# Turned results for latent and cross attention in a two-layer hybrid decoder trunk

## The chip, the cores and the metric

The kernel runs on one core of a Trainium2 chip. The metric is the device time of one execution in microseconds (us). Three timed runs of the kernel before lie between 2052.78 and 2055.78 us, with a median of 2054.7 us. All arithmetic is float32 or a float32 value split into two fp32r parts.

## The reference

Two layers work on a residual stream of 512 tokens by 1024 features. Each layer has three attention branches that are gated and summed, and a squared-ReLU MLP.

```python
h = rmsnorm(x, g_mix[l])
dq, dk, dv, c_q, c_kv_kr, xq, gate_logits = jnp.split(h @ w_in[l], split_idx, axis=-1)
y_diff = diff_attention(...) @ w_diff_o[l]      # 8 heads, two maps a head, values 128 wide, causal
y_mla = latent_attention(...) @ w_mla_o[l]      # 8 heads, q and k 96 wide, values 64 wide, causal
y_mem = memory_cross_attention(...) @ w_cross_o[l]   # 4 heads, 128 wide, 256 memory tokens
x = x + (sig(g0) * y_diff + sig(g1) * y_mla + sig(g2) * y_mem) @ w_out[l]
x = x + jnp.square(jax.nn.relu(rmsnorm(x, g_mlp[l]) @ w_mlp1[l])) @ w_mlp2[l]
```

In each attention `p = softmax(q k^T * scale)` over the keys and `o = p v`. The change touches how `o` is made in latent attention (called mla in the kernel) and in cross attention; differential attention keeps its way.

## The kernel before

**Tiling.** Tokens are cut into four blocks of 128 (`NT = 4`, `P = 128`). Large products are made in split form: an operand is held as `hi`, its value rounded to fp32r, and `lo`, the rest; `mm3` (L108 to L111) makes three fp32r matmuls, hi·hi, hi·lo and lo·hi, into one PSUM bank. A split takes one ScalarE copy for `hi` (L101 or, with a scale, L105) and one VectorE subtraction for `lo` (L102 or L106). Weights stream in by SyncE DMAs of up to 512 KB and are split the same way in `do_split`. Attention products (L609, L612, L638, L642) are partly plain float32: the trace shows a plain float32 matmul as two instructions, each with its own weight load, and a transpose as one.

**Order.** `layer(l)` makes a list of entries. `phases` (L850) holds the attention units of a stage, `PLAN` (L25) the projections that stand beside them, and `merge` (L45) deals the two out in turn. Stage 1 has the first two pairs of latent heads (`mla_att(0)`, `mla_att(1)`) beside four gate products (`gx`) and the memory projection (`mem`). Stage 2 has the other two pairs beside `xq` and the first differential pair `d0`. Stage 3 has the four cross heads beside `d1` and `ym`. The framework then orders the instructions of each engine ahead of time, by priority and by its own model of durations; on the chip every engine runs its list in that fixed order and waits on semaphores.

**Attention before.** `attend` (L596) serves all three kinds. It makes the scores of two maps into PSUM (`ps("s")`), masks them, takes the negated maximum, and writes `exp` with its row sums into a tile `P` (L626). Then blocks of 128 by 128 of `P` are transposed on TensorE into a bank of `ps("tp")` (L638), copied out by ScalarE into a `PT` tile (L640, which is L95), and each block is the stationary operand of a plain float32 matmul whose moving operand is a block of values (L642): 64 columns wide for latent heads, 128 for cross and differential ones. The result has tokens on the partitions. After a head (cross) or a pair of heads (latent) `o_copy` (L659) copies the 512 columns out, `o_finish` (L644) divides by the row sums on VectorE (L646), transposes the result back in four blocks (L649) and splits it into fp32r `hi` and `lo` for the output projection.

**Values before.** `kvb_item` (L483) writes the values of four latent heads as one float32 tile for each two token blocks (L494, VectorE), `mem_chunk` the memory values likewise (L364, ScalarE).

**Buffers.** Tile pools at L72 to L74: `B` has 22 slots of 128 by 512 and holds, among others, latent keys and queries (four slots each for half the heads), values, the latent `ckv` and `cq`, memory inputs, keys and values, `xq` and the differential operands. `PT` has 2 slots, `P` 2, `ps("tp")` 2 and `ps("o")` 1. A tile's first write waits until a slot is free.

Of the kernel before, what the change touches and what calls it, by code (L numbers as in the profile page):

```python
# [59 lines left out]
def tile_trunk(ctx: ExitStack, tc: tile.TileContext, x_t, mem_t, mem_n, pos, ifr, gcol, grow, w_ck, w_cq, w_kvb, w_qb,  # L60
# [11 lines left out]
    pools = {n: pool(n, b) for n, b in (("H", 16), ("O", 16), ("X", 8), ("G", 1), ("B", 22), ("scr", 5), ("PT", 2))}  # L72
    p_p = pool("P", 2)
# [34 lines left out]
    def mm3(o, l, r, first, last):  # L108
        T.matmul(o, lhsT=l[0], rhs=r[0], start=first, stop=False)  # L109
        T.matmul(o, lhsT=l[0], rhs=r[1], start=False, stop=False)  # L110
        T.matmul(o, lhsT=l[1], rhs=r[0], start=False, stop=last)  # L111
# [28 lines left out]
    def trig():  # L140
# [44 lines left out]
        G.dma_start(out=lvt.rearrange("p (l d) -> p l d", l=L), in_=grow[:, 128:384].partition_broadcast(P))  # L185
# [93 lines left out]
    def layer(l):  # L279
# [58 lines left out]
        def mem_chunk(c):  # L338
            def done(tp, q):
# [143 lines left out]
        def kvb_item(hf):  # L483
            def fn(w):
                kn = [tl("O") for _ in range(2)]
                vv = [tl("B") for _ in range(2)]
                kc = []
                for t in range(NT):
# [5 lines left out]
                    V.tensor_scalar(vv[t // 2][:, sl], q[:, 256:512], s["skv"][:, t:t + 1], None, ALU.mult)  # L494
# [101 lines left out]
        def attend(N, qk, causal, o_out, ssum, vs, diff):  # L596
# [30 lines left out]
            nb = N // P  # L627
# [5 lines left out]
            blocks = [(m, j) for m in range(1 if diff else 2) for j in range(nb)]  # L633
            for i in range(0, len(blocks), 4):
                bl = blocks[i:i + 4]
                tp_ = ps("tp")
                for n, (m, j) in enumerate(bl):
                    T.transpose(tp_[:, n * P:(n + 1) * P], in_=pt[:, m, j * P:(j + 1) * P], identity=ident)  # L638
                w = tl("PT")
                copy_to(w[:, :len(bl) * P], tp_[:, :len(bl) * P])  # L640
                for n, (m, j) in enumerate(bl):
                    T.matmul(o_out[m], lhsT=w[:, n * P:(n + 1) * P], rhs=vs[m](j), start=j == 0, stop=j == nb - 1)  # L642
# [334 lines left out]
```

## Time and profile before

| what | value |
|---|---|
| three timed runs, median | 2054.7 us |
| the same, lowest and highest | 2052.78 and 2055.78 us |
| span of the profiled execution, first to last instruction | 2047.5 us |
| TensorE busy | 2025.8 us, 99% of the span |
| weight loads busy | 1735.7 us, 85% |
| VectorE busy | 1125.5 us, 55% |
| ScalarE busy | 870.5 us, 43% |

What lies around the span is not recorded for the profiled execution; the median of the timed runs is 7.2 us above its span. Matmuls are pipelined and their ends are modelled, so the duration in a row says how long one is in the array, and the distance from one start to the next says what it costs. PE in the rows is the TensorE matmul, PEld its weight load, DVE is VectorE, ACT is ScalarE, POOL is GpSimd, and an engine name with a q is its queue issuing a DMA.

### The profile page before, as it was taken

To read this page: it belongs to the slowest core of one execution; us is meant where nothing else is said; L and a number is where in the kernel's file an instruction comes from. 1 tells how busy PE (TensorE), PEld (TensorE's weight loads), DVE (VectorE), ACT (ScalarE), POOL (GpSimd) and SP (SyncE) were. 2 spreads that over 40 slices of the span, in tenths; PEclk is the share of its full clock that TensorE was granted. 3 is DMA by queue.
4 is the path that set the end of the run, shared out by engine and by line. 5 is a ranking of instruction groups with operands and counts; after the bars stand their busy time and mean duration, and the time that the engine had idled before them with its cause. 6 is when DMAs were issued, how large, how long until landed. Compare 5 with 4: busy or idle time off the path is not lost.

```text
span 2047.5 us, 28283 instructions
## 1 busy us (share of the span) xinstructions
PE 2025.8 (99%) x11280; PEld 1735.7 (85%) x11280; DVE 1125.5 (55%) x2058; ACT 870.5 (43%) x1607; POOL 152.4 (7%) x125
## 2 busy tenths in 40 slices
PE   8999999999999999999999999999999999999999
PEld 7889997888878888888888999978897788888887
DVE  7754665667656443443457546657685554434442
ACT  6565543444443442322345645444454334323221
POOL 2300110101100000000003001101020000000000
PEclk9999999999999999999999999999999999999999
DMA  5242122222214333333333321212222233333332
GB/s 178 78 140 74 63 65 60 73 73 63 73 48 150 96 97 94 102 93 101 118 95 94 115 72 63 67 58 73 73 63 63 92 124 93 94 102 93 101 94 73
DMA packets 54036, 181.09 MB, mean 88 GB/s; under 512 B 6176, under 2 KB 6704, under 8 KB 53904
## 3 DMA queue, kind: packets, MB, share of 16 engines
q1 hardware_dynamic: 51840, 175.66, 28.0%
q10 hardware_dynamic: 1872, 3.21, 0.5%
q8 instruction: 89, 1.46, 0.3%
q0 software_dynamic: 192, 0.41, 0.1%
q14 instruction: 43, 0.35, 0.1%
HBM read 175.06 MB, written 4.19 MB: 88 GB/s over the span
## 4 chain that ended last, share of the span: by engine, by line
PE 97%; ACT 1%; DMA 1%; DVE 1%; issue 0%; SPq 0%; POOL 0%; POOLq 0%; ACTq 0%
PE psacc L109 21%; PE psacc L110 20%; PE psacc L111 20%; PE pss L109 7%; PE pss L110 7%; PE pss L111 7%; PE pso L642 4%; PE pss L609 3%; PE pss L612 2%; PE pstp L638 2%; PE pstp L649 1%; PE pstp L590 1%; PE pstp L478 1%; DMA X<-in_x_t_dram 0%; DMA B<-in_mem_n_dram 0%; PE pstp L236 0%
## 5 line engine op out<-in xcount | busy, mean ns | idle before, releaser
L101 ACT ACTIVATE whi<-wraw 128x1024 fp32r<-128x1024 f32 (+3 forms) x320 | 334.5, 1047 | 726.8 <-PE psacc L110 354.5
L102 DVE TENSOR_TENSOR wlo<-wraw,whi 128x1024 fp32r<-128x1024 f32 (+3 forms) x320 | 386.0, 1207 | 103.1 <-ACT whi L101 101.8
L109 PE MATMUL psacc<-H,whi 128*128 128x512 f32 x816 | 322.0, 395 | 1.3 <-ACT B L560 1.3
L110 PE MATMUL psacc<-H,whi 128*128 128x512 f32 x816 | 321.1, 393 | 0.0
L111 PE MATMUL psacc<-H,wlo 128*128 128x512 f32 x816 | 319.6, 392 | 0.0
L109 PE MATMUL psacc<-whi,H 128*128 128x256 f32 (+1 forms) x928 | 272.8, 295 | 7.2 <-ACT whi L101 5.8
L110 PE MATMUL psacc<-wlo,H 128*128 128x256 f32 (+1 forms) x928 | 265.9, 287 | 0.5 <-DVE wlo L102 0.5
L111 PE MATMUL psacc<-whi,H 128*128 128x256 f32 (+1 forms) x928 | 265.4, 287 | 0.0
L109 PE MATMUL pss<-O,whi 128*128 128x512 f32 x640 | 249.4, 391 | 1.6 <-ACT O L105 1.6
L110 PE MATMUL pss<-O,whi 128*128 128x512 f32 x640 | 249.7, 390 | 0.0
L111 PE MATMUL pss<-O,wlo 128*128 128x512 f32 x640 | 249.4, 390 | 0.0
L109 PEld LDWEIGHTS psacc<-whi,H 128*128 128x128 f32 x928 | 176.9, 191 | 15.6 <-ACT whi L101 6.0
L109 PEld LDWEIGHTS psacc<-H,whi 128*128 128x128 f32 x816 | 153.3, 188 | 34.7 <-ACT B L560 1.7
L110 PEld LDWEIGHTS psacc<-H,whi 128*128 128x128 f32 x816 | 153.3, 188 | 32.4 <-issue 1.5
L111 PEld LDWEIGHTS psacc<-H,wlo 128*128 128x128 f32 x816 | 153.3, 188 | 32.4 <-issue 1.5
L110 PEld LDWEIGHTS psacc<-wlo,H 128*128 128x128 f32 x928 | 177.6, 191 | 3.2 <-issue 1.4
L111 PEld LDWEIGHTS psacc<-whi,H 128*128 128x128 f32 x928 | 177.0, 191 | 0.0
L808 DVE TENSOR_TENSOR X<-psacc,X 128x512 f32<-128x512 f32 x64 | 44.3, 692 | 207.1 <-PE psacc L111 207.1
L109 PEld LDWEIGHTS pss<-O,whi 128*128 128x128 f32 x640 | 120.0, 188 | 28.3 <-ACT O L105 2.0
L110 PEld LDWEIGHTS pss<-O,whi 128*128 128x128 f32 x640 | 120.2, 188 | 25.2 <-DVE O L106 0.5
L111 PEld LDWEIGHTS pss<-O,wlo 128*128 128x128 f32 x640 | 120.2, 188 | 24.5
L626 ACT ACTIVATE P<-pss,nmx 128x128 f32<-128x128 f32 (+2 forms) x224 | 115.2, 521 | 51.3 <-DVE nmx L623 44.0
(223 smaller groups left out, 3139.6 us busy)
## 6 DMA issues: line engine op xcount, KB each, us to landing
wraw<-in_w_dram SPq DMA_DIRECT2D x128, 512.0 KB, 3.6
wraw<-in_w_g_dram SPq DMA_DIRECT2D x48, 512.0 KB, 3.6
wraw<-in_w_d_dram SPq DMA_DIRECT2D x48, 512.0 KB, 3.8
wraw<-in_w_mem_dram SPq DMA_DIRECT2D x16, 512.0 KB, 3.9
wraw<-in_w_od_dram SPq DMA_DIRECT2D x16, 512.0 KB, 3.5
wraw<-in_w_out_dram SPq DMA_DIRECT2D x16, 512.0 KB, 3.8
X<-in_x_t_dram SPq DMA_DIRECT2D x16, 256.0 KB, 6.3
wraw<-in_w_xq_dram SPq DMA_DIRECT2D x8, 512.0 KB, 3.8
```

What stands on the lines that cost most here:

```text
L101: A.activation(out=hi, in_=src, func=AF.Copy)
L102: V.tensor_tensor(out=lo, in0=src, in1=hi, op=ALU.subtract)
L109: T.matmul(o, lhsT=l[0], rhs=r[0], start=first, stop=False)
L110: T.matmul(o, lhsT=l[0], rhs=r[1], start=False, stop=False)
L111: T.matmul(o, lhsT=l[1], rhs=r[0], start=False, stop=last)
L478: T.transpose(tp_[:96, t * P:(t + 1) * P], in_=src[t][:, h * 96:(h + 1) * 96], identity=ident)
L609: T.matmul(sw[m][:, :max(N, 256)], lhsT=qk[m][0][a], rhs=qk[m][1][b], start=i == 0, stop=i == 2)
L612: T.matmul(sv[m], lhsT=qk[m][0], rhs=qk[m][1], start=True, stop=True)
L626: A.activation(out=pt[:, m, :N], in_=sv[m], func=AF.Exp, bias=nmx[:, m:m + 1], accum_out=ssum[m])
L638: T.transpose(tp_[:, n * P:(n + 1) * P], in_=pt[:, m, j * P:(j + 1) * P], identity=ident)
L642: T.matmul(o_out[m], lhsT=w[:, n * P:(n + 1) * P], rhs=vs[m](j), start=j == 0, stop=j == nb - 1)
L808: V.tensor_tensor(out=xt, in0=q, in1=xt, op=ALU.add)
```

## The change

Latent and cross attention leave the common `attend`. It becomes `scores`, which ends with the tile of exponentials; differential attention goes on with `pv_tok`, the old transposes and plain matmuls. The other two go on with three new steps:

- `scaled` takes the reciprocals of two row sums (VectorE) and multiplies the exponentials by them, one ScalarE pass in place for each map.
- `turned` transposes two to four blocks into one bank of `ps("tp")` and splits them into fp32r `hi` and `lo` of up to 512 columns.
- the values, now split, are the stationary operand of `mm3`, and the turned probabilities the moving one. The result has features on the partitions and tokens along the columns, as the output projection wants it, so it is split straight from PSUM; the division and the four transposes back are gone.

For latent heads two token blocks go together: the unit of an even block leaves its tile in `s["pe"]`, and the unit of the odd block makes the products for both blocks and both heads of the pair. A stationary operand of 128 columns holds the values of both heads, so half of each 512-wide result (one head's values by the other head's probabilities) is not used. In the last key block of a pair only the odd token block counts, and the matmul is 256 wide, written to two runs of 128 columns of the bank.

Values are made split: in `kvb_item` a ScalarE copy and a VectorE step in place of one VectorE step, in `mem_chunk` a VectorE step beside the ScalarE one. The pools grow (`B` 22 to 24, `PT` 2 to 4, `P` 2 to 3), the scratch of the software DMA ring shrinks to 2048 bytes, and the four small loads that GpSimd issued are issued by ScalarE.

```diff
-    pools = {n: pool(n, b) for n, b in (("H", 16), ("O", 16), ("X", 8), ("G", 1), ("B", 22), ("scr", 5), ("PT", 2))}
-    p_p = pool("P", 2)
+    pools = {n: pool(n, b) for n, b in (("H", 16), ("O", 16), ("X", 8), ("G", 1), ("B", 24), ("scr", 5), ("PT", 4))}
+    p_p = pool("P", 3)
...
-    G.dma_start(out=posi, in_=pos)
+    A.dma_start(out=posi, in_=pos)
-    G.dma_start(out=fr, in_=ifr.partition_broadcast(P))
+    A.dma_start(out=fr, in_=ifr.partition_broadcast(P))
-    G.dma_start(out=gr, in_=grow[:, 0:128].partition_broadcast(P))
+    A.dma_start(out=gr, in_=grow[:, 0:128].partition_broadcast(P))
...
-        G.dma_start(out=lvt.rearrange("p (l d) -> p l d", l=L), in_=grow[:, 128:384].partition_broadcast(P))
+        A.dma_start(out=lvt.rearrange("p (l d) -> p l d", l=L), in_=grow[:, 128:384].partition_broadcast(P))
...
-                    o = tl("B")
+                    hi, lo = tl("B", F32R), tl("B", F32R)
                     for t in range(2):
-                        A.activation(out=o[:, t * 256:(t + 1) * 256], in_=q[:, t * 256:(t + 1) * 256], func=AF.Copy, scale=mst["r"][:, t:t + 1])
-                    s["mv"].append(o)
+                        sl = slice(t * 256, (t + 1) * 256)
+                        split_scaled(hi[:, sl], lo[:, sl], q[:, sl], mst["r"][:, t:t + 1])
+                    s["mv"].append((hi, lo))
...
-                vv = [tl("B") for _ in range(2)]
+                vv = [(tl("B", F32R), tl("B", F32R)) for _ in range(2)]
...
-                    V.tensor_scalar(vv[t // 2][:, sl], q[:, 256:512], s["skv"][:, t:t + 1], None, ALU.mult)
+                    split_scaled(vv[t // 2][0][:, sl], vv[t // 2][1][:, sl], q[:, 256:512], s["skv"][:, t:t + 1])
...
+        def scaled(pt, N, ssum):
+            rc = small("rc", 2, 6)
+            V.reciprocal(out=rc, in_=ssum)
+            for m in range(2):
+                scale_to(pt[:, m, :N], pt[:, m, :N], rc[:, m:m + 1])
+
+        def turned(blocks):
+            tp_ = ps("tp")
+            n = len(blocks) * P
+            for i, b in enumerate(blocks):
+                T.transpose(tp_[:, i * P:(i + 1) * P], in_=b, identity=ident)
+            hi, lo = tl("PT", F32R), tl("PT", F32R)
+            split_into(hi[:, :n], lo[:, :n], tp_[:, :n])
+            return hi, lo
...
+                    pt = scores(256, [(s["xq", c][hh][:, q * P:(q + 1) * P], kk) for q in (2 * qp, 2 * qp + 1)], False, [cs[:, m:m + 1] for m in range(2)], False)
+                    scaled(pt, 256, cs)
+                    w = turned([pt[:, m, j * P:(j + 1) * P] for j in range(2) for m in range(2)])
+                    for j in range(2):
+                        mm3(s["co"][:, qp * 256:(qp + 1) * 256], tuple(z[:, j * 256 + hh * P:j * 256 + (hh + 1) * P] for z in s["mv"][c]), tuple(z[:, j * 256:(j + 1) * 256] for z in w), j == 0, j == 1)
                     if qp == 1:
-                        f = small("of", 8, 3)
-                        V.reciprocal(out=f[:, :4], in_=s["cs"][:, :4])
-                        o_finish(o_copy(), f[:, :4], 4, None, "oc")
+                        o_split("oc")
...
+                    pt = scores(N, qk, True, [cs[:, m:m + 1] for m in range(2)], False)
+                    scaled(pt, N, cs)
+                    if qi % 2 == 0:
+                        s["pe"] = pt
+                        return
+                    pair = (s["pe"], pt)
+                    o = ps("o")
+                    ov = o.rearrange("p (m q t) -> p m q t", m=2, q=2)
+                    for j in range(qi + 1):
+                        g = 1 if j == qi else 0
+                        w = turned([x[:, m, j * P:(j + 1) * P] for m in range(2) for x in pair[g:]])
+                        f = (j % 2) * 256 + h0 * 64
+                        mm3(ov[:, :, 1, :] if g else o, tuple(z[:, f:f + P] for z in s["v", hf][j // 2]),
+                            tuple(z[:, :256] if g else z for z in w), j == 0, j == qi, skip_group_check=True)
+                    if qi == 1:
+                        s["oT"] = tl("O", F32R), tl("O", F32R)
+                    hi, lo = s["oT"]
+                    sl = slice((qi - 1) * P, (qi + 1) * P)
+                    for m in range(2):
+                        r = slice(m * 64, (m + 1) * 64)
+                        split_into(hi[r, sl], lo[r, sl], o[r, m * 256:(m + 1) * 256])
...
-    nc = _bacc.Bacc("TRN2", target_bir_lowering=False, num_devices=1)
+    nc = _bacc.Bacc("TRN2", target_bir_lowering=False, num_devices=1, dynamic_dma_scratch_size=2048)
```

## Rows read from the trace of the kernel before

**Rows 1.** The page: the span, TensorE's busy time, the busy tenths of TensorE and its granted clock in 40 slices of the span, and the shares of the chain of work that ended last.

```profile
span 2047.5 us, 28283 instructions
...
PE 2025.8 (99%) x11280; PEld 1735.7 (85%) x11280; DVE 1125.5 (55%) x2058; ACT 870.5 (43%) x1607; POOL 152.4 (7%) x125
...
PE   8999999999999999999999999999999999999999
...
PEclk9999999999999999999999999999999999999999
...
PE 97%; ACT 1%; DMA 1%; DVE 1%; issue 0%; SPq 0%; POOL 0%; POOLq 0%; ACTq 0%
```

**Rows 2.** TensorE's waits over the whole span: who waited for whom, us in total, times, longest.

```profile
PE psacc L109 <- ACT whi L101: 5.8, 2, 5.6
PE pstp L649 <- DVE scr L646: 2.8, 4, 0.8
```

**Rows 3.** Groups of TensorE's instructions, shapes kept apart: line, engine, operation, tiles, shape, count, then busy us and mean ns of one.

```profile
L642 PE MATMUL pso<-B,PT 128*128 128x128 f32 x448 | 64.1, 277 | 0.7 <-ACT PT L95 0.7
...
L642 PE MATMUL pso<-B,PT 128*128 128x64 f32 x320 | 40.7, 268 | 0.7 <-ACT PT L95 0.7
...
L649 PE MATMUL pstp<-ident,scr 128*128 128x128 f32 x128 | 19.6, 275 | 2.8 <-DVE scr L646 2.8
```

**Rows 4.** TensorE in order of time in a stretch of layer 0's stage 1 (start us, us, what, count): a run of 64-wide products, then split products of 256 columns (29 in a row start from 135.65 to 139.00), then the four transposes back.

```profile
133.75 1.90 PE L642 MATMUL pso<-B,PT 128*128 128x64 f32 x16
135.45 0.36 PE L111 MATMUL psacc<-whi,O 128*128 128x256 f32 x1
135.65 0.28 PE L109 MATMUL psacc<-whi,O 128*128 128x256 f32 x1
...
139.00 0.28 PE L110 MATMUL psacc<-wlo,O 128*128 128x256 f32 x1
...
139.36 0.60 PE L649 MATMUL pstp<-ident,scr 128*128 128x128 f32 x4
139.80 0.38 PE L638 MATMUL pstp<-ident,P 128*128 128x128 f32 x2
```

**Rows 5.** The same view in a stretch of layer 1's cross stage: eight 128-wide instructions of L642 and what follows them.

```profile
1279.37 1.06 PE L642 MATMUL pso<-B,PT 128*128 128x128 f32 x8
1280.18 0.36 PE L111 MATMUL psacc<-whi,H 128*128 128x256 f32 x1
1280.38 0.28 PE L109 MATMUL psacc<-whi,H 128*128 128x256 f32 x1
```

**Rows 6.** The same view where split products of 512 columns follow each other: 21 in a row start from 97.98 to 102.52, these are the first and the last.

```profile
97.98 0.39 PE L109 MATMUL psacc<-H,whi 128*128 128x512 f32 x1
...
102.52 0.39 PE L111 MATMUL psacc<-H,wlo 128*128 128x512 f32 x1
```

**Rows 7.** Busy time of the engines (instructions in brackets) in the stretches of latent and cross attention of layer 0 and of layer 1.

```profile
118.30:300.00 181.70, 179.96 (x1418) 171.82 (x1417) 104.37 (x198) 100.94 (x224) 23.88 (x15) 1.00 0.27 85
1136.00:1330.00 194.00, 193.51 (x1490) 183.86 (x1489) 110.25 (x204) 103.84 (x225) 23.01 (x14) 1.00 0.25 76
```

**Rows 8.** Groups of ScalarE instructions, shapes kept apart, in the shapes that the change adds or removes, or the nearest.

```profile
L626 ACT ACTIVATE P<-pss,nmx 128x512 f32<-128x512 f32 x48 | 32.9, 690 | 14.9 <-DVE nmx L623 14.9
...
L659 ACT ACTIVATE scr<-pso 128x512 f32<-128x512 f32 x32 | 19.1, 598 | 73.0 <-PE pso L642 72.6
...
L364 ACT ACTIVATE B<-psacc,rmem 128x256 f32<-128x256 f32 x8 | 3.3, 473 | 0.6 <-PE psacc L111 0.6
```

**Rows 9.** The same view of VectorE: the division on the result, and the subtraction of a split out of PSUM.

```profile
L646 DVE TENSOR_TENSOR scr<-scr,of 128x512 f32<-128x512 f32 x32 | 22.1, 689 | 56.7 <-ACT scr L659 46.1 <-POOL of L132 10.6
...
L102 DVE TENSOR_TENSOR O<-pstp,O 128x512 fp32r<-128x512 f32 x16 | 11.0, 686 | 11.8 <-ACT O L101 11.8
```

**Rows 10.** ScalarE in order of time at the start: its DMA issue, a table load, and its first pass.

```profile
0.74 0.41 ACTq L123 DMA_DIRECT2D gc<-in_gcol_dram  x1
1.18 1.28 ACT L223 ACT_TABLE_LOAD   x1 [1.18 <-PEq L965]
3.74 0.63 ACT L223 ACTIVATE scr<-X 128x512 f32<-128x512 f32 x1 [1.28 <-DMA X<-in_x_t_dram]
```

**Rows 11.** TensorE in order of time in layer 0 between the last gate product of stage 1 and the first product of the memory projection.

```profile
120.78 0.39 PE L111 MATMUL psacc<-H,wlo 128*128 128x512 f32 x1
121.42 0.66 PE L642 MATMUL pso<-B,PT 128*128 128x64 f32 x4 [0.25 <-ACT PT L95]
...
126.35 1.10 PE L642 MATMUL pso<-B,PT 128*128 128x64 f32 x8 [0.47 <-ACT PT L95]
...
128.81 0.39 PE L109 MATMUL psacc<-whi,O 128*128 128x256 f32 x1 [0.52 <-ACT O L105]
```

**Rows 12.** ScalarE and its queue in order of time around there: the last two tiles of latent queries, and the loads of the memory tokens, which need slots of `B`.

```profile
113.47 0.68 ACT L98 ACTIVATE B<-pstp,gc 96x512 f32<-96x512 f32 x1 [2.78 <-PE pstp L478]
113.91 0.33 ACTq L205 DMA_DIRECT2D B<-in_mem_n_dram  x1
...
120.37 0.63 ACT L206 ACTIVATE B<-B 128x512 f32<-128x512 f32 x1 [2.86 <-DMA B<-in_mem_n_dram]
...
126.75 0.42 ACTq L323 DMA_DIRECT2D B<-in_mem_t_dram  x1
```

More of the change, by code (lines that the diff above doesn't have):

```diff
@@ L106, in split_scaled, with mm3 @@
         V.scalar_tensor_tensor(out=lo, in0=src, scalar=col, in1=hi, op0=ALU.mult, op1=ALU.subtract)
[L108 to L111, printed above, removed]
+    def mm3(o, l, r, first, last, **kw):
+        T.matmul(o, lhsT=l[0], rhs=r[0], start=first, stop=False, **kw)
+        T.matmul(o, lhsT=l[0], rhs=r[1], start=False, stop=False, **kw)
+        T.matmul(o, lhsT=l[1], rhs=r[0], start=False, stop=last, **kw)
     ident = ct("ident", [P, P])
@@ L594, in diff_chunk, with scores @@
             return chunk256(w_d[l, c, p], x_h, 4, done)
-        def attend(N, qk, causal, o_out, ssum, vs, diff):
+        def scores(N, qk, causal, ssum, diff):
             if N <= 256 and not diff:
@@ L626, in attend @@
                 A.activation(out=pt[:, m, :N], in_=sv[m], func=AF.Exp, bias=nmx[:, m:m + 1], accum_out=ssum[m])
-            nb = N // P
             if diff:
@@ L632, in attend, with pv_tok, o_split @@
                 V.scalar_tensor_tensor(out=pt[:, 0, :N], in0=pt[:, 1, :N], scalar=c, in1=pt[:, 0, :N], op0=ALU.mult, op1=ALU.add)
[L633 to L642, printed above, removed]
+            return pt
+        def pv_tok(pt, nb, o, vs):
+            tp_ = ps("tp")
+            for j in range(nb):
+                T.transpose(tp_[:, j * P:(j + 1) * P], in_=pt[:, 0, j * P:(j + 1) * P], identity=ident)
+            w = tl("PT")
+            copy_to(w[:, :nb * P], tp_[:, :nb * P])
+            for j in range(nb):
+                T.matmul(o, lhsT=w[:, j * P:(j + 1) * P], rhs=vs(j), start=j == 0, stop=j == nb - 1)
+        def scaled(pt, N, ssum):
[4 more added lines that the diff above has]
+        def turned(blocks):
+            tp_ = ps("tp")
+            n = len(blocks) * P
[4 more added lines that the diff above has]
+            return hi, lo
+        def o_split(key):
+            hi, lo = tl("O", F32R), tl("O", F32R)
+            split_into(hi, lo, s["co"])
+            s.setdefault(key, []).append((hi, lo))
         def o_finish(o, f, ng, gain, key):
@@ L650, in o_finish @@
             hi, lo = tl("O", F32R), tl("O", F32R)
-            if gain is None:
-                split_into(hi, lo, tp_)
-            else:
-                split_scaled(hi, lo, tp_, gain)
+            split_scaled(hi, lo, tp_, gain)
             s.setdefault(key, []).append((hi, lo))
@@ L713, in fn @@
                     vf = lambda j: v_[j // 2][:, (j % 2) * 256 + hh * P:(j % 2) * 256 + (hh + 1) * P]
-                    attend(N, qk, True, [o[:, qi * P:(qi + 1) * P]], [cs[:, m, qi:qi + 1] for m in range(2)], [vf], True)
+                    pt = scores(N, qk, True, [cs[:, m, qi:qi + 1] for m in range(2)], True)
+                    pv_tok(pt, qi + 1, o[:, qi * P:(qi + 1) * P], vf)
                     if qi == NT - 1:
```

18 lines of the change are left out of this document (4 added, 14 removed).

## The prediction

> **What bounds the kernel now.** I read the page first: TensorE is busy in 99% of the span, 97% of the chain that ended last is TensorE's, and its granted clock is the full one, 2.4 GHz, in all 40 slices [rows 1]. Busy says little where matmuls are pipelined, so I went to the waits next: the longest total that TensorE lost to one cause is 5.8 us, nearly all of it the first weight split at the start [rows 2]. Then the timeline, to see what one matmul costs from start to start. The reader is to see there that neighbours follow each other at a steady distance. So TensorE's list of instructions is the kernel's length, and a change is worth what it takes out of or puts into that list, unless it opens a wait. VectorE and ScalarE are half idle in the stages that are changed: 104.4 and 100.9 of 181.7 us in layer 0, 110.3 and 103.8 of 194.0 us in layer 1 [rows 7].
>
> **Prices on TensorE.** The duration in a row (277 or 268 ns for L642, whether 128 or 64 columns move) [rows 3] is time in the array, not cost. Starts give the cost. Sixteen 64-wide instructions of L642 take 135.45 - 133.75 = 1.70 us, and the next split product starts 0.20 us before its successor where 0.12 is usual, so 0.08 more belongs to them: (1.70 + 0.08)/16 = 0.111 us [rows 4]. Eight 128-wide ones: (0.81 + 0.08)/8 = 0.111 us [rows 5]. Without the 0.08, which another run of plain instructions behind them may hide, it is 0.106 and 0.101. I take 0.108. The reader is to see that 64 columns cost the same as 128: narrow plain products pay for something other than their columns. Four transposes back take 139.80 - 139.36 = 0.44 us, 0.11 each [rows 4]. A split product of 256 columns costs (139.00 - 135.65)/28 = 0.120 us [rows 4], one of 512 columns (102.52 - 97.98)/20 = 0.227 us [rows 6].
>
> **What goes.** Latent heads: 2 layers x 4 pairs x 2 heads x 10 blocks are 160 plain products, two instructions each, the 320 of the 64-wide group [rows 3]. Cross heads: 2 x 4 x 2 units x 4 blocks are 64 products, 128 of the 448 instructions of the other group; the remaining 320 are differential attention's and stay. Transposes back: 32 results x 4 are the 128 of L649 [rows 3]; 8 latent pairs and 8 cross heads lose theirs, 64. Sum: 448 x 0.108 + 64 x 0.11 = 48.4 + 7.0 = 55.4 us.
>
> **What comes.** For a latent pair, blocks (0,1) make one 512-wide triple and one 256-wide, blocks (2,3) make three and one: 12 instructions of 512 and 6 of 256. Eight pairs: 96 and 48. A cross unit makes two 256-wide triples, 16 units: 96. Sum: 96 x 0.227 + 144 x 0.120 = 21.8 + 17.3 = 39.1 us. The transposes of the probabilities are as many as before. Scores are untouched.
>
> **Net on TensorE:** 55.4 - 39.1 = 16.3 us less. With 0.111 for L642 it is 17.7, with 0.101 to 0.106 (128 x 0.101 + 320 x 0.106 = 46.8) 14.7.
>
> **A bound on one new form.** In the last key block of a pair the result goes to two runs of 128 columns; no row of before writes so. As a whole 256-wide product it costs 0.120, as two 128-wide ones 2 x 0.111 = 0.222; 48 of them make 0 to 4.9 us more. I take 0, since the columns in a run are contiguous and the instruction is one. The Trainium skill (PSUM — Partial Sum Buffer, Specifications) says that any non-contiguous access pattern slows matmuls significantly; by that rule these 48 go to the upper end, and no run here shows it yet. It is a rival below.
>
> **Work on the other engines.** ScalarE gains two scaling passes a unit. A 256-wide pass with a scale is 0.473 us and a 512-wide one with a bias 0.690 [rows 8], so at the latent heads' mean width of 320 about 0.53. A latent pair: 8 x 0.53 + 4 result copies x at most 0.473 - the copy out of 0.598 and a `hi` copy of the like = +4.9, eight pairs 39 us. A cross head: 4 x 0.473 - 0.598 = +1.3, eight heads 10 us. Values of 16 blocks: 16 x 0.473 = 8 us. About 57 us in both layers. VectorE: a subtraction of 512 columns is 0.686, the division removed 0.689 [rows 9]; one of 256 columns lies between half of that and the whole, I take 0.5. A latent pair: 4 x 0.686 + 6 x 0.5 - 0.689 - 0.686 = +4.4, eight pairs 35 us; a cross head 2 x 0.686 - 0.689 = +0.7, eight 6 us; memory values 8 x 0.5 = 4 us. About 45 us. Half of each falls into a layer, so in layer 0's stretch VectorE comes to (104.4 + 22)/181.7 = 70% and ScalarE to (100.9 + 28)/181.7 = 71%. Both stay under TensorE, so I cost them at nothing; what hides them are the projections that `merge` deals between the units. If that cover is gone they stand on the path.
>
> The Trainium skill (TensorEngine Tiling (Array Packing), PSUM Bottleneck) warns that once TensorE is faster the copies out of PSUM may become the limit, and advises sharing them between ScalarE and VectorE. The shares just worked out speak against a limit here; it is weighed below.
>
> **Waits.** The chain of one unit grows. Between `exp` and the transposes come a reciprocal and two scalings, about 1.2 us; between the transposes and the products the `lo` subtraction, about 0.7 us, and queue time on both engines. A bank of `tp` stays taken that much longer; behind it queue transposes of the projections (L357, L391, L590). The doubled `PT` still holds two pairs of tiles, the third `P` holds the even block's tile. Slots of `B` get tighter: latent values need 8 tiles where they needed 4, the pool gains 2. Values, keys and queries of all latent heads take 24 of 24 slots, where they took 20 of 22. In layer 0 the loads of the memory tokens, which need slots, are issued from ScalarE's queue just when the last query tiles are written [rows 12], and TensorE has no projection between 121.4 and 128.8 us [rows 11]; it lives on attention units there and loses 0.25, 0.47 and 0.52 us in visible waits. If the loads come later, this hole grows. I take it as it is: the third `P` tile lets scores go ahead and free key and query slots earlier, which works the other way.
>
> **The start.** Three more DMA issues stand on ScalarE's queue ahead of its table load, 0.41 us each by the one that is there, 1.2 us; ScalarE idles 1.28 us for its first input after the load [rows 10], which hides them. Bounds: 0 to 1 us later if the broadcasts take longer to issue. I take 0. The fourth, in the rotary tables' step, waits for a `B` slot with ScalarE's passes queued behind it; nothing is short of slots that early. GpSimd loses these issues and waits for none of them.
>
> **Sum.** 2047.5 - 16.3 = 2031.2 us of span; on the median of the timed runs 2054.7 - 16.3 = 2038.4 us. Timed runs of one kernel lie 3 us apart, so about 0.2%, 4 us, is what can be told from no change.
>
> **Rivals.**
> 1. *The list shrinks and waits give part of it back.* The hole of [rows 11] is 7.4 us of attention units. Their chains are longer by about 2 us a step; with two exposed steps in a layer, and one more delay where the second half's value tiles wait for the `ckv` tiles to be read, it is 3 to 6 us a layer, 6 to 12 in all: 2044 to 2050. For it speaks the full pool, against it that layer 1 has no such memory statistics and that the pool is not shorter in stages 3 and 4.
> 2. *Slower: slots of `B` keep the memory projection out of stage 1.* If its four input tiles get slots only once a pair of heads is through, two latent pairs run without cover in each layer. A pair has four rounds through transposes, two copies and products after its scores; at some 3 us a round plus 5 us for scores and exponentials that is 17 us of chain with 9 us of TensorE work in it, so 8 us idle a pair, 4 pairs, 32 us: 2054.7 - 16.3 + 32 = 2070. It gives no gain from about 16 us of idleness on. Against it: keys and queries of a pair come free when its scores are made, not when the pair ends, and scores can run ahead.
> 3. *Strided results cost double:* 2038.4 + 4.9 = 2043.
> 4. *More than the list.* Differential attention keeps small waits (2.8 us in front of L649 alone) [rows 2]; with three `P` and four `PT` tiles and another order some of these go: 2032 to 2035.
> 5. *The change doesn't do what it says,* the new triples costing what the old products cost: 2054.7 - 7.0 for the transposes = 2048.
>
> **How the numbers follow.** Forecast 2038.4, with 2034 to 2042 for it, 0.55. Rival 1 0.15, rival 3 0.06, rival 4 0.10, rival 5 0.05, rival 2 and lesser forms of it 0.09. Range 2032 to 2050: it takes in the forecast and rivals 1, 3, 4 and 5 and leaves out rival 2 and the edges. Faster by over 0.2% (under 2050.6): all but rival 2 and a little of rival 1, 0.85. Within: 0.07. Slower: 0.08.
>
> **What would show it.** Right: 11280 - 448 - 64 + 240 = 11008 matmuls; triples 0.227 and 0.120 us apart also where the stationary operand is values; each stretch of [rows 7] about 8 us shorter; everything after it only shifted; TensorE's waits still a few us. Wrong: waits of L109 to L111 for `PT` tiles or of transposes for `tp` banks, longer holes at the start of stage 1, 256-wide triples over 0.2 us apart in the last key block (rival 3), or VectorE or ScalarE over 85% in these stretches.

## The result, and the profile after

| | runs | median us | lowest to highest |
|---|---|---|---|
| before | 4 | 2054.36 | 2052.78 to 2055.78 |
| after | 4 | 2038.57 | 2037.26 to 2039.67 |

The medians are 15.8 us apart. The ratio on record, 0.9934 with a 95% interval of 0.9919 to 0.9949, puts the gain at some 10 to 17 us. The forecast was 2038.4. The median came out within 0.2 us of it, but the experiments show that this is a sum of terms of which several were wrong and cancelled.

The profiled execution of after took 2039.67 us, the longest of its four, with a span of 2037.6 us: 9.9 us less than the span of before, which was at the low end of before's runs. In every run of this case the time lies 1.7 to 2.1 us above its own span. What I called "around the span" ahead of the prediction (7.2 us) was mostly the distance between one short execution and the median of others. That execution held the full clock throughout; of the 64 later runs of before, those with a mean granted clock of 0.999 or 1.000 took 2048.6 to 2053.3 us and those with 0.998 or less 2052.5 to 2058.8. Spans are compared with spans below, medians with medians.

The page of after (span, busy time, three of its lines of 40 slices, chain), against [rows 1]:

```profile
span 2037.6 us, 27922 instructions
...
PE 2005.1 (98%) x11008; PEld 1715.9 (84%) x11008; DVE 1162.2 (57%) x2170; ACT 917.4 (45%) x1727; POOL 146.0 (7%) x121
...
PE   8999999999999999999999999999999999999999
...
PEclk9989999999999999999999999999999999999999
...
PE 95%; ACT 2%; DVE 1%; DMA 1%; issue 0%; POOL 0%; ACTq 0%; DVEq 0%; POOLq 0%
```

The count of matmuls is the one worked out, 11008. VectorE gained 36.7 us and ScalarE 46.9 (I had about 45 and 57). The reader is to look at the third slice of the clock: an 8 where before has 9, and it stands at 102 to 153 us, layer 0's stage 1. ScalarE now holds 2% of the chain.

The groups of TensorE with the new products and those next to them (columns as in [rows 3]):

```profile
L642 PE MATMUL pso<-B,PT 128*128 128x128 f32 x320 | 46.2, 276 | 0.0
...
L610 PE MATMUL pss<-B,B 64*128 64x256 f32 x192 | 28.6, 310 | 0.0
...
L610 PE MATMUL pss<-B,B 64*128 64x512 f32 x96 | 21.5, 428 | 0.3 <-ACT P L627 0.3
...
L610 PE MATMUL pss<-B,B 64*128 64x384 f32 x96 | 18.7, 370 | 0.0
...
L109 PE MATMUL pso<-PT,B 128*128 128x256 f32 x48 | 14.7, 307 | 0.0
...
L109 PE MATMUL pso<-PT,B 128*128 128x512 f32 x32 | 13.7, 428 | 2.0 <-ACT PT L101 2.0
...
L669 PE MATMUL pstp<-ident,scr 128*128 128x128 f32 x64 | 9.7, 275 | 2.1 <-DVE scr L666 2.1
```

The plain 64-wide products are gone, 320 of the 128-wide ones and 64 transposes back are left, and the triples are there in the numbers worked out (96 of 512 and 144 of 256 columns over the lines L109 to L111). The group that nobody touched is the surprise: L610, the scores of differential attention, was L609 before with the same 192, 96 and 96 instructions and was busy 33.6, 28.3 and 23.9 us, now 28.6, 21.5 and 18.7, at the same mean duration of one. Before:

```profile
L609 PE MATMUL pss<-B,B 64*128 64x256 f32 x192 | 33.6, 313 | 0.0
L609 PE MATMUL pss<-B,B 64*128 64x512 f32 x96 | 28.3, 431 | 0.0
L609 PE MATMUL pss<-B,B 64*128 64x384 f32 x96 | 23.9, 370 | 0.0
```

The prices of the new triples, in order of time in layer 0 (start us, us, what, count):

```profile
150.12 0.28 PE L109 MATMUL pso<-PT,B 128*128 128x256 f32 x1
150.24 0.28 PE L109 MATMUL psacc<-whi,O 128*128 128x256 f32 x1
150.36 0.28 PE L110 MATMUL psacc<-wlo,O 128*128 128x256 f32 x1
150.48 0.28 PE L110 MATMUL pso<-PT,B 128*128 128x256 f32 x1
150.59 0.28 PE L111 MATMUL pso<-PT,B 128*128 128x256 f32 x1
150.71 0.28 PE L111 MATMUL psacc<-whi,O 128*128 128x256 f32 x1
```

In this stretch the `pso` products are those of a last key block, written to two runs of 128 columns. They start 0.11 to 0.12 us ahead of the next instruction, like the contiguous products among them.

**Where the time went.** To split the 9.9 us, I gave every matmul of either trace the usual distance to its successor for its form (0.227 and 0.120 us for split products, 0.111 and 0.108 for the narrow plain ones, 0.109 for transposes, and so on). The sum of these is the "list"; what the starts are apart beyond that is "excess", and holds waits and stretches at half clock.

| us | before | after | difference |
|---|---|---|---|
| first matmul starts at | 5.6 | 6.8 | +1.2 |
| list | 1987.5 | 1970.8 | -16.7 |
| excess behind differential scores (L609, L610) | 13.2 | 1.0 | -12.2 |
| other excess, 0 to 300 us | 7.5 | 21.3 | +13.8 |
| other excess, 1060 to 1300 us | 0.9 | 7.2 | +6.3 |
| other excess, the rest | 28.6 | 26.5 | -2.1 |

These add to -9.7, the difference of the spans but for 0.2. The list does what was worked out, -16.3; two terms of some 12 and 20 us stand against each other that were not in the sum. Of the 13.8 us in layer 0, 8.7 lie at 125 to 150 us (10.2 of excess, before 1.5). Windows there (columns as in [rows 7]):

```profile
130.00:135.00 5.00, 4.83 (x14) 3.16 (x13) 3.40 (x9) 5.00 (x16) 0.00 (x0) 0.66 0.46 156
135.00:140.00 5.00, 2.42 (x14) 1.79 (x13) 3.49 (x11) 3.92 (x10) 0.70 (x1) 0.82 0.72 224
140.00:145.00 5.00, 5.00 (x25) 5.00 (x25) 3.81 (x9) 4.66 (x13) 0.00 (x0) 0.50 0.04 16
...
125.00:150.00 25.00, 20.25 (x99) 16.84 (x98) 13.55 (x32) 19.22 (x51) 0.70 (x1) 0.80 0.33 108
```

TensorE idles 4.75 of the 25 us. The other half of the 10.2 us doesn't show as idleness: from 140 to 145 us it is busy throughout, but at a granted clock of 0.50, the level of 1.2 GHz, and gets 25 instructions done. The windows of 5 us mix two levels; cut more finely, the clock is at the lower level in two stretches:

```profile
131.50:134.80 3.30, 3.30 (x10) 2.10 (x8) 2.62 (x7) 3.30 (x13) 0.00 (x0) 0.50 0.52 174
...
138.30:145.00 6.70, 5.89 (x27) 5.89 (x28) 5.09 (x12) 6.09 (x16) 0.00 (x0) 0.50 0.26 89
```

Ten us at half clock are 5 us of TensorE's time, an estimate that agrees with the 5.5 us of excess that are not idleness. What stood still is seen in order of time, TensorE first and then ScalarE:

```profile
127.41 0.38 PE L654 MATMUL pstp<-ident,P 128*128 128x128 f32 x2
129.79 0.50 PE L109 MATMUL pso<-PT,B 128*128 128x512 f32 x1 [2.01 <-ACT PT L101]
...
139.11 0.58 PE L109 MATMUL psacc<-whi,O 128*128 128x256 f32 x1 [2.58 <-ACT O L105]
```

```profile
124.73 0.35 ACTq L205 DMA_DIRECT2D B<-in_mem_n_dram  x1
125.26 0.19 ACT L206 ACTIVATION_READ_ACCUMULATOR B<-B 128x1 f32 x1
128.53 0.63 ACT L206 ACTIVATE B<-B 128x512 f32<-128x512 f32 x1 [3.09 <-DMA B<-in_mem_n_dram]
128.54 0.33 ACTq L205 DMA_DIRECT2D B<-in_mem_n_dram  x1
129.07 0.19 ACT L206 ACTIVATION_READ_ACCUMULATOR B<-B 128x1 f32 x1
129.16 0.58 ACT L101 ACTIVATE PT<-pstp 128x512 fp32r<-128x512 f32 x1
...
135.51 0.82 ACTq L323 DMA_DIRECT2D B<-in_mem_t_dram  x2
```

ScalarE stands 3.09 us on a square of memory tokens (L206) whose load it issued itself only at 124.73. Right behind it in its queue is the `PT` copy for which TensorE waits 2.01 us. ScalarE then works through what has queued up, 5.00 of the 5 us from 130 to 135. The four loads of the next inputs (L323) are issued from 135.5 to 136.9, where before they were issued from 125.4 to 126.8 ([rows 12] shows the last), and the memory projection, which waits 2.58 us for the first split of these inputs, starts at 139.11 instead of 128.81 [rows 11].

A smaller wait stands where the latent values are made. In the new way VectorE's part of their split (L106) comes behind ScalarE's part, and a later product waits longer for the PSUM bank that they read. TensorE's waits of after, and the one of before in that place:

```profile
PE psacc L109 <- DVE B L106: 5.7, 4, 1.7
```

```profile
PE psacc L109 <- DVE B L494: 0.4, 2, 0.2
```

One of 1.35 us stands in each layer where before has 0.20. The longest, 1.7, is not the split values' alone: the kernel before with larger pools (e5 below) has 1.4 there.

### The profile page after: what moved, and what is told of

Read it like the earlier page. It is cut to its first block, busy times and chain, and to the rows that moved or that the text cites. A ratio compares the mean times of both kernels' runs of the same rounds, so it can differ in the third digit from the quotient of the medians.

```text
span 2037.6 us, 27922 instructions
## 1 busy us (share of the span) xinstructions
PE 2005.1 (98%) x11008; PEld 1715.9 (84%) x11008; DVE 1162.2 (57%) x2170; ACT 917.4 (45%) x1727; POOL 146.0 (7%) x121
## 4 chain that ended last, share of the span: by engine, by line
PE 95%; ACT 2%; DVE 1%; DMA 1%; issue 0%; POOL 0%; ACTq 0%; DVEq 0%; POOLq 0%
PE psacc L109 21%; PE psacc L111 20%; PE psacc L110 20%; PE pss L109 7%; PE pss L111 7%; PE pss L110 7%; PE pss L610 2%; PE pss L613 2%; PE pso L642 2%; PE pstp L654 1%; PE pstp L638 1%; PE pstp L591 1%; PE pso L110 1%; PE pso L111 1%; PE pso L109 1%; PE pstp L479 1%
## 5 line engine op out<-in xcount | busy, mean ns | idle before, releaser
L109 PE MATMUL psacc<-H,whi 128*128 128x512 f32 x816 | 321.6, 394 | 2.6 <-ACT B L561 2.2
L111 PE MATMUL psacc<-H,wlo 128*128 128x512 f32 x816 | 320.1, 392 | 0.0
L109 PE MATMUL psacc<-whi,H 128*128 128x256 f32 (+1 forms) x928 | 271.6, 294 | 10.3 <-ACT whi L101 6.8
L111 PE MATMUL psacc<-whi,H 128*128 128x256 f32 (+1 forms) x928 | 264.3, 287 | 0.2 <-DVE H L106 0.2
L109 PE MATMUL pss<-O,whi 128*128 128x512 f32 x640 | 249.8, 392 | 1.6 <-ACT O L105 1.6
L111 PE MATMUL pss<-O,wlo 128*128 128x512 f32 x640 | 250.5, 392 | 0.0
L109 PEld LDWEIGHTS psacc<-whi,H 128*128 128x128 f32 x928 | 177.6, 192 | 17.8 <-ACT whi L101 6.8
L109 PEld LDWEIGHTS psacc<-H,whi 128*128 128x128 f32 x816 | 153.2, 188 | 36.0 <-ACT B L561 2.6
L111 PEld LDWEIGHTS psacc<-H,wlo 128*128 128x128 f32 x816 | 153.2, 188 | 33.6 <-issue 2.0
L111 PEld LDWEIGHTS psacc<-whi,H 128*128 128x128 f32 x928 | 177.3, 192 | 1.0 <-DVE H L106 0.4
L109 PEld LDWEIGHTS pss<-O,whi 128*128 128x128 f32 x640 | 120.4, 188 | 27.3 <-ACT O L105 2.0
L111 PEld LDWEIGHTS pss<-O,wlo 128*128 128x128 f32 x640 | 121.0, 189 | 24.9
```

The lines of the kernel that those rows point to most:

```text
L109: T.matmul(o, lhsT=l[0], rhs=r[0], start=first, stop=False, **kw)
L111: T.matmul(o, lhsT=l[1], rhs=r[0], start=False, stop=last, **kw)
```

## The experiments

My theory after the result was that the list had shrunk as worked out and that layer 0's stage 1 gave back about 10 us because ScalarE stands on the memory loads. The rivals were that slots of `B` hold the stage up, that the side edits (loads, scratch, pools) and not the new products make the gain, and that the framework lays out the whole order anew around any edit.

"Before" is run again on the same chip beside each kernel; its medians were 2050.4 for e1 to e4, 2050.5 for e5 to e8, 2051.0 for e9 to e11 and 2050.8 for e12.

**The side edits alone, on the kernel before.** e1 moves the four loads, e2 shrinks the scratch of the software DMA ring.

```diff
-    G.dma_start(out=posi, in_=pos)
+    A.dma_start(out=posi, in_=pos)      # e1, and likewise fr, gr, lvt
-    nc = _bacc.Bacc("TRN2", target_bir_lowering=False, num_devices=1)
+    nc = _bacc.Bacc("TRN2", target_bir_lowering=False, num_devices=1, dynamic_dma_scratch_size=2048)   # e2
```

> The kernel before with one edit: its four small loads are issued by ScalarE, none by GpSimd; the scratch of the software DMA ring stays as it is. Theory A: a kernel without any software DMA spends about 6 us less around its span (the changed kernel's four runs lie 2.0 us above their spans, the one profiled before 5 to 8 us), so about 6 us less around the span, about 1 us more at the start, 2049 to 2050 us against 2054.4. Theory B: the 15.8 us of the change come from TensorE's list alone, and the place of four loads is nothing: 2054 to 2055. Theory C: the smaller scratch does it, not the loads: 2054 to 2056 here.

> The kernel before with one edit: the scratch of the software DMA ring is 2048 bytes; GpSimd goes on issuing the four loads. Theory A (the software DMAs themselves cost the time around the span): 2054 to 2055. Theory C (the scratch does it): 2048 to 2050. Theory B: 2054 to 2055.

e1: 2054.26 us, ratio 1.0018 (1.0008 to 1.0028). e2: 2050.36, ratio 0.9995 (0.9985 to 1.0005). The scratch does nothing, and nothing is hidden in time around the span. The moved loads cost: the first matmul starts at 6.9 instead of 5.6 us, and the rest of the 3.9 us between the medians wasn't taken apart.

**The loads and the memory statistics, on the kernel after.** e3 gives one load, that of the positions, back to GpSimd. e4 emits layer 0's memory statistics earlier, behind the queries of the latent branch.

```diff
-    A.dma_start(out=posi, in_=pos)
+    G.dma_start(out=posi, in_=pos)      # e3
-        e += [... cq_item(2), Entry(lambda w: cq_finish())]
-        pre = ([Entry(lambda w: mem_stats())] if l == 0 else []) + [Entry(mem_begin)]
+        e += [... cq_item(2), Entry(lambda w: cq_finish())] + ([Entry(lambda w: mem_stats())] if l == 0 else [])   # e4
+        pre = [Entry(mem_begin)]
```

> The changed kernel with one edit undone: the load of the positions (2 KB) goes back to GpSimd as its only software DMA. Theory A: one software DMA brings the whole 6 us around the span back, 2043 to 2045 us. Theories B and C: 2038 to 2039.

> The changed kernel with one edit: the statistics of the memory tokens (four loads and four squares on ScalarE, layer 0 only) stand in the program right after the latent query input, ahead of stage 0's value and query items, instead of ahead of the memory projection. Theory D: TensorE's hole at 125 to 145 us (waits of 2.0 and 2.6 us and matmuls at the half clock behind them) comes from ScalarE standing in order on the squares of loads that land one after the other while TensorE needs its copy of turned probabilities: the hole goes, 2030 to 2034 us. Theory E: it comes from slots of the pool B being short because of the split values, and the loads would be late anyway: 2037 to 2039.

e3: 2027.07 us, ratio 0.9880 (0.9863 to 0.9897), far from what any theory expected. Its first matmul starts at 6.9 us, so the start isn't what it wins. The framework laid TensorE's list out anew around the edit: the order differs in many places, and the excess falls from 56.0 to 44.9 us, 6.2 of that in the first 300 us. e4: 2035.71, ratio 0.9922 (0.9908 to 0.9937), between what its two theories expected. The hole at 125 us shrinks from 10.2 to 3.2 us of excess, but one of 8.6 opens at 50 to 75 us, where a product waits 6.1 us for the split of the values (B L106). The hole moved rather than went.

**The halves of the change.** e5 is the kernel before with all side edits and the larger pools; e6 adds the latent half, e7 the cross half; e8 is the changed kernel once more.

```diff
 # e6: cross attention as before, latent attention as after
-                    scaled(pt, 256, cs)
-                    w = turned([pt[:, m, j * P:(j + 1) * P] for j in range(2) for m in range(2)])
...
+                    pv_old(pt, 2, [s["co"][:, q * P:(q + 1) * P] for q in qs], [vf, vf])
 # e7: latent attention as before, cross attention as after
-                    scaled(pt, N, cs)
...
+                    pv_old(pt, qi + 1, [o[:, qi * P + m * 64:qi * P + (m + 1) * 64] for m in range(2)], vs)
```

> The kernel before with the change's surroundings alone: pools B 24, PT 4 and P 3, the scratch of 2048 bytes and the four loads on ScalarE; attention and values as before. In the changed kernel's trace the 384 score matmuls of differential attention (64 rows each) take 62.5 us from start to start where before they take 74.7, because 116 of them start within 60 ns of their neighbour where before it is 64. Theory F: the larger pools do that (a third P tile lets both maps' score banks be free at once), so this kernel, too, shows over 100 close pairs and is 8 to 13 us under the kernel with moved loads alone (2054.3): 2041 to 2047, about 0.996 of before. Theory G: it comes with the new attention code and its order: 64 close pairs, 2053 to 2056.

> The changed kernel with cross attention undone: cross heads go the old way through plain products, division and four transposes back, and memory values are one float32 tile. Theory A (TensorE's list): the list has 5.8 us more than the changed kernel's (128 x 0.108 + 32 x 0.11 - 96 x 0.120), so 5 to 7 us over the changed kernel in the same call; the holes in stage 1 of both layers stay. Theory H (holes weigh more than the list and come from cross attention's memory values in part): at most 2 us over it, or under it.

> The changed kernel with latent attention undone: latent heads go the old way, latent values are one float32 tile for each two blocks. By TensorE's list alone it has 10.5 us more than the changed kernel (320 x 0.108 + 32 x 0.11 - 96 x 0.227 - 48 x 0.120). Theory A with holes: the holes of stage 1 (about 13 us in layer 0 and 6 us in layer 1 over what before has there) belong to the latent part, so they go and the kernel is as fast as the changed one or up to 8 us faster. Theory I (the holes come from the moved loads and the pools): 8 to 12 us slower than the changed kernel.

> The changed kernel as it is, for a comparison on one chip with the others of this call: 0.993 to 0.994 of before.

| | median us | ratio | span | list | excess | of it behind L609/L610 |
|---|---|---|---|---|---|---|
| e5, pools and side edits | 2042.61 | 0.9957 (0.9945 to 0.9969) | 2040.7 | 1987.5 | 42.1 | 5.6 |
| e6, and latent | 2053.12 | 1.0006 (0.9996 to 1.0016) | 2055.3 | 1977.0 | 67.4 | 7.9 |
| e7, and cross | 2030.34 | 0.9895 (0.9882 to 0.9908) | 2030.0 | 1981.3 | 37.8 | 0.6 |
| e8, both | 2036.79 | 0.9925 (0.9913 to 0.9937) | 2035.4 | 1970.8 | 53.7 | 1.0 |

Three things follow. The pools win 0.43% together with the side edits (and more without the moved loads, which cost e1 0.18%), with the list unchanged: 7.6 of the 8.1 us of excess that go lie behind differential scores. The cross half wins what its list says and more: spans -10.7, list -6.2, and 5.0 of the rest again behind differential scores. And the latent half, which carries the larger part of the forecast, *loses* on top of the cross half: its list is 10.5 us shorter, its excess 15.9 longer, and the median 6.45 us later. (e6, the latent half without the cross half, is 10.5 us later than e5; 9.8 us of its excess stand at 350 to 375 us at a granted clock of 0.73, so that profile is not all stage 1, and at 16.3 us over e8 it lies outside what either theory expected.) Not all of the memory projection's delay is the latent half's: it starts at 134.29 us in e5 and at 135.21 in e7. In e7 the statistics' loads follow each other just as they do in the changed kernel, but TensorE has plain products to go on with, and its clock stays at the full level:

```profile
135.00:140.00 5.00, 4.79 (x35) 4.31 (x35) 3.12 (x9) 3.66 (x11) 0.70 (x1) 1.00 0.50 177
140.00:145.00 5.00, 5.00 (x45) 5.00 (x45) 3.68 (x7) 3.82 (x10) 0.00 (x0) 1.00 0.01 3
```

Against the same windows of after: 45 instructions against 25 from 140 to 145 us. The mixes differ, but the same split products of 256 columns start 0.21 us apart there in after and 0.12 in e7.

**Which buffer, which wait.** e9 is the changed kernel with two more slots of `B`, paid for with one weight buffer less; e10 emits the statistics behind the first value item; e11 is e5 with the third `P` tile alone (`B` 22, `PT` 2).

```diff
-    RB, NB = 3, 4
+    RB, NB = 2, 4                                     # e9, with ("B", 24) -> ("B", 26)
-        pre = ([Entry(lambda w: mem_stats())] if l == 0 else []) + [Entry(mem_begin)]
-        K0, K1, Q0, Q1 = [kvb_item(0)], ...
+        pre = [Entry(mem_begin)]                      # e10
+        K0, K1, Q0, Q1 = [kvb_item(0)] + ([Entry(lambda w: mem_stats())] if l == 0 else []), ...
```

> The changed kernel with two more slots in B (26), paid for by one buffer less for raw weights (2 in place of 3). Theory J: the latent half's holes (0 to 300 us and 1060 to 1300 us, together 28 us over the plain list, against 11 in the kernel with cross attention alone changed) come from B being full when the memory loads want slots: with two free slots the holes shrink to 10 to 16 us and it is 2022 to 2032, unless the shorter weight buffer opens waits of its own on whi. Theory K: they come from the order of ScalarE's passes (loads' squares, copies out of PSUM) and from the longer chain of a unit: 2035 to 2042.

> The changed kernel with the statistics of the memory tokens moved to stand after the first value item of stage 0 (layer 0 only), a place with projections before and behind. Theory D (ScalarE stands in order on those loads just when stage 1 needs it): the hole at 125 to 150 us shrinks from 11 us to 3 as in the other place that was tried, and no hole opens at 50 to 75 us this time: 2026 to 2031. Theory L: it moves again: 2034 to 2038.

> The kernel before with moved loads, small scratch and a third P tile, B at 22 and PT at 2. Theory F1 (the third P tile lets both maps' score banks come free together): about 104 close pairs of score matmuls and 2041 to 2045, as with all three pools larger. Theory F2 (it is PT): 64 close pairs, 2052 to 2055.

e9: 2032.32 us, ratio 0.9904 (0.9891 to 0.9917). With the slots the median is about 4.5 us under e8's, between what the two theories expected, of the 16 us in question, and the excess at 125 to 150 us stays at 8.7. e10: 2036.41, ratio 0.9924 (0.9912 to 0.9936): 3.2 at 125 us, but 12.7 at 75 to 100, where ScalarE stands on the same squares and TensorE waits 8.1 us behind it. ScalarE of e10:

```profile
81.95 0.63 ACT L206 ACTIVATE B<-B 128x512 f32<-128x512 f32 x1 [2.72 <-DMA B<-in_mem_n_dram]
81.96 0.33 ACTq L205 DMA_DIRECT2D B<-in_mem_n_dram  x1
...
84.57 0.63 ACT L206 ACTIVATE B<-B 128x512 f32<-128x512 f32 x1 [0.96 <-DMA B<-in_mem_n_dram]
84.58 0.33 ACTq L205 DMA_DIRECT2D B<-in_mem_n_dram  x1
...
87.05 0.63 ACT L206 ACTIVATE B<-B 128x512 f32<-128x512 f32 x1 [1.76 <-DMA B<-in_mem_n_dram]
```

The reader is to see the pattern: each load is issued 10 ns after a square starts, and the next square stands until it has landed, some 2.5 us after its issue. In each of the three places where the block was put (after, e4, e10), ScalarE stands there. e11: 2047.58, ratio 0.9977 (0.9966 to 0.9988), with as many close pairs of differential scores as e5 (104; before has 64). The third `P` tile alone, beside the side edits, makes the pairs. The time missed the 2041 to 2045 that went with them: the profiled execution of e11 has a stretch at lower clock with 9.3 us of excess at 1350 to 1375 us, so the size of its effect on the median is not settled by it.

**The loads issued together.** e12 is the changed kernel with the four loads issued one behind the other behind the entry with the latent branch's statistics, and the squares where e4 had them ("the queries of the cross attention" in the expectation are the latent ones).

```diff
+    def mem_loads():
+        mst["t"] = [tl("B") for _ in range(4)]
+        for i, mt in enumerate(mst["t"]):
+            A.dma_start(out=mt, in_=mem_n[(i // 2) * P:(i // 2 + 1) * P, (i % 2) * 512:(i % 2 + 1) * 512])
...
-        for t in range(2):
-            for j in range(2):
-                mt, junk = tl("B"), tl("B")
-                A.dma_start(out=mt, ...)
-                A.activation(out=junk, in_=mt, func=AF.Square, ...)
+        for i, mt in enumerate(mst["t"]):
+            junk = tl("B")
+            A.activation(out=junk, in_=mt, func=AF.Square, ...)
```

> The changed kernel with layer 0's four memory-token loads issued together as soon as the latent results are emitted, and their squares emitted after the queries of the cross attention. Theory D2 (the hole at 125 to 150 us is ScalarE standing on loads that land one after the other; issued together, well ahead of the squares, they have landed): the hole shrinks to about 3 us and none opens at 50 to 100 us: 2026 to 2031. Theory L (the hole goes to another place, since the planner lays the list out anew around any edit): 2034 to 2038.

e12: 2027.39 us (2026.35 to 2029.43), ratio 0.9889 (0.9873 to 0.9906). The loads are issued at 31.7 to 34.4 us and land 4.2 to 4.8 us later, the squares run at 44.1 to 46.0, and ScalarE waits for none of them. The excess at 125 to 150 us is 3.1, and none opens at 50 to 100 us (4.4 in all, as in the changed kernel). Windows of e12:

```profile
130.00:135.00 5.00, 3.60 (x17) 1.94 (x17) 4.22 (x11) 4.94 (x14) 0.00 (x0) 1.00 0.28 105
135.00:140.00 5.00, 5.00 (x38) 4.70 (x38) 3.92 (x10) 4.95 (x15) 0.00 (x0) 1.00 0.00 0
140.00:145.00 5.00, 5.00 (x40) 4.84 (x39) 3.21 (x6) 4.02 (x10) 0.00 (x0) 1.00 0.00 0
...
125.00:150.00 25.00, 23.52 (x157) 20.16 (x156) 16.85 (x33) 20.83 (x50) 0.00 (x0) 1.00 0.27 93
```

The theory of the loads holds for layer 0. The median alone wouldn't show it, since e3 came to 2027.07 by another order with the serial loads left in; the place shows it: of the 10.9 us of excess that e12 has less than e8, 10.0 lie in the first 300 us and 8.1 at 125 to 150. The span of 2024.5 us is the shortest of the profiled executions. It is 5.5 us under e7's 2030.0, but e12's profiled execution was its fastest and e7's its slowest; the medians are 3 us apart, and by the ratios (0.9889 and 0.9895) the two can't be told apart. So with the loads out of the way the latent half no longer costs; that it gains is not shown, and e7 with the loads issued together was not run.

## Why the prediction was right, and where only its total was

- **The list: right.** -16.7 us by the traces, -16.3 forecast, with the counts as worked out. (Its lower variant is 14.8 by the unrounded terms, not 14.7.) Starts, not durations, give the cost: the new 512-wide products last 428 ns in their row and cost 0.233 to 0.236 us to the next start (median), near the 0.227 of the old ones.
- **Rival 3, two runs of columns: wrong.** These products keep the distance of 0.11 to 0.12 us. The Trainium skill (PSUM — Partial Sum Buffer, Specifications) says that any non-contiguous access pattern slows matmuls significantly; here the measurement decides against it for runs of 128 columns.
- **The start: I took 0, it costs 1.2 us.** The bound ended at 1. "ScalarE idles 1.28 us, which hides them" was the failed step: e1, which has nothing but the moved loads, starts about as late as the changed kernel (6.9 and 6.8 us). The issues themselves are over at 2.6 us, a microsecond before the input lands; what is lost is the table load, which before ran ahead of that wait [rows 10] and now stands behind it:

```profile
3.62 1.28 ACT L105 ACT_TABLE_LOAD   x1 [3.62 <-DMA X<-in_x_t_dram]
```

- **The other engines: the step "both stay under TensorE, so I cost them at nothing" failed,** and with it "I take it as it is" on the hole of [rows 11]. Their mean share was not near a limit: 19.22 of 25 us on ScalarE in the hole itself. What counts is the order in ScalarE's queue: a square that waits 3.09 us for its own load holds up the `PT` split behind it, on which the turned products hang, and only with what queues up behind the square is ScalarE full for some microseconds. With the old way (e7) there are 2.6 us of excess in that place, with the new way 10.2, half of that through the clock. This is rival 1's mechanism, a wait and a longer chain at the start of stage 1: 13.8 us in layer 0 and 6.3 in layer 1, the latter only in part explained, instead of 6 to 12 in all. e12 shows what the cause at 125 to 150 us is; slots of `B`, on which rivals 1 and 2 leaned, are about 4.5 us (e9). The split of the values, whose cost on TensorE was put at nothing too, makes TensorE wait 1.35 us for a PSUM bank where it waited 0.20, in each layer.
- **Rival 4 came true too, and larger than priced.** I had read differential attention's small waits in front of L649, 2.8 us; the gain of 12 us is not in any wait. It is in the scores, where matmuls on rows 0 to 63 (one map) and 64 to 127 (the other) start together (within 60 ns): 116 pairs instead of 64. Two pairs of 256-wide scores of after, in order of time:

```profile
314.26 0.50 PE L610 MATMUL pss<-B,B 64*128 64x256 f32 x2
...
329.36 0.39 PE L610 MATMUL pss<-B,B 64*128 64x256 f32 x2
```

  The first two follow each other and are done in 0.50 us, the second two start 4 ns apart and are done in 0.39, what the first of the other two takes by itself (0.381). The Trainium skill (TensorEngine Tiling (Array Packing), Key Properties) says that different tiles of the array can execute matmuls in parallel; the trace agrees: 110 of the 116 pairs start within 17 ns of each other. With a third `P` tile the pairs appear (e5, e11), by my reading since both maps' scores are then ready at the same time. Three 256-wide scores by themselves in before, and six in after, each with what follows:

```profile
337.77 0.61 PE L609 MATMUL pss<-B,B 64*128 64x256 f32 x3
338.31 0.50 PE L110 MATMUL psacc<-H,whi 128*128 128x512 f32 x1
```

```profile
501.12 0.63 PE L610 MATMUL pss<-B,B 64*128 64x256 f32 x6
501.68 0.94 PE L642 MATMUL pso<-B,PT 128*128 128x128 f32 x6
```

  Six cost what three did (0.56 and 0.54 us), and the three cost more than their 3 x 0.120. So each group of scores, with other matmuls before and behind it, pays something on top of its products, and part of the gain is that 76 such groups are left of 102.
- **So the total was right by cancellation:** -16.7 for the list, -12.2 for the scores, +18.0 for other excess, +1.2 for the start. The last 6 us of the difference of the medians are not in the two profiles: the profiled execution of before lies about 5 us under its median, that of after 1.1 above. That the median met the forecast within 0.2 us is luck: beside before on another chip (e8) the medians are 13.7 us apart.

Three points stay open. What the latent half is worth with its loads issued together is not settled (e12 against e7). In layer 1, 6.3 us more excess stand at 1060 to 1300 us without any memory statistics; e9 shifts it little (5.6). Of it, TensorE's waits show 1.35 us for the values' split (0.20 before) and 0.97 for the first split of the memory inputs (none before), and the granted clock is 0.50 from 1148.7 to 1152.0; the rest wasn't taken apart. And e3 shows that the move of one small load changes the framework's order enough to be worth 10 us; in e3 the serial loads are still there (ScalarE stands 2.93 us on a square, excess 7.8 at 125 us), so its gain is not e12's. Whether the two add was not tried.

## What to carry to other kernels

Price a change by starts in TensorE's list, but then ask of every engine that gains work what stands ahead of it in its fixed queue: a pass that waits for a load issued one step earlier on the same queue is a wait for everything behind it, and a cover that hid it before may be the very work that the change removes. Issue such loads together and well ahead. And look at what a larger pool does for parts that the change doesn't touch: here the larger pools won 8 us with the side edits against them, and a change measured in one piece gets the credit for them.

## What the runs showed of the hardware

- A stretch with gaps costs twice: around waits of 2.01 and 2.58 us, with few products between them, the granted clock of after was 0.50 from 131.5 to 134.8 us and from 138.3 to 145.0, and split products of 256 columns started 0.21 us apart instead of 0.12. In e12, with waits of at most 0.97 us in the same place, it stayed at 1.00. The half-clock part of the excess was about as large as the idle part (5.5 and 4.75 us).
- Scores of 64 rows on the two halves of the array start within 17 ns of each other in 110 of 116 close pairs. The 384 scores took 74.7 us from start to start before and 62.5 after, at the same duration of one.
- A table load on ScalarE (1.28 us) that ran while the first input was on its way cost nothing; placed behind that wait it delayed TensorE's first matmul from 5.6 to 6.8 us.
